# A two-layer DiT in one kernel: opening strips reordered and halved, roots on ScalarE, layer 0's row sums by a matmul with ones, joint and end in half banks

## The chip, the cores and the metric

The kernel runs on one NeuronCore of a Trainium2 chip. The metric is the device time of one execution in microseconds (us). The engines are named as the profile names them: PE (TensorE matmul) and PEld (its weight loads), DVE (VectorE), ACT (ScalarE), POOL (GpSimd), SP (the queue that issues most loads).

## The reference, cut to what matters

Width 2048, 256 tokens of `x` and 256 of `ctx`, all in float32. Layer 0 mixes by a Fourier transform, layer 1 by windowed attention with a prefix; after layer 1 only `x` is kept and normalised once more.

```python
def _rmsnorm(x, g):
    return x * lax.rsqrt(jnp.mean(x * x, axis=-1, keepdims=True) + EPS) * g

for i in range(2):
    shift, scale, gate = split(silu(c) @ ada_w[i] + ada_b[i], 3)         # the same for ctx with c_ctx
    h  = _rmsnorm(x,  norm_g[i]) * (1 + scale)   + shift
    hc = _rmsnorm(xc, norm_g[i]) * (1 + scale_c) + shift_c
    # layer 0: u, z = h @ w_in; y = mix(real(fft2(u))) * silu(z)
    # layer 1: attention over h and hc, y = attention * silu(z)
    x  = x + gate * (y @ w_out[i])
    xc = xc + gate_c * (yc @ w_out[i])                                   # layer 0 only
return _rmsnorm(x, final_g)
```

## The kernel before

Every float32 product is made of three matmuls in a reduced type (`mm3`, lines 74 to 76): both operands are split into a high part (a cast on ACT, line 61) and a low part (a subtraction on DVE, line 62), and high x high, high x low and low x high are added up in PSUM. The small exact products (transposes, the modulation `ada`) are plain float32 matmuls. PSUM has eight banks of 128 x 512. Weights arrive as 128 x 2048 strips of 1 MB through the pool `raw` (three buffers, in the opening two more called `raw2`); SP issues each load as soon as its buffer is free.

**Order of work.** The program text is only a wish. A scheduler lays out the instructions of each engine's queue from estimated times, in the order of the text where it can; `tc.issue_after(ins)` pins what its block issues on the engine of `ins` behind `ins`. The queues are then run in order.

**The opening** (up to about 150 us). The four strips `xn0` to `xn3` are 128 token rows each (two of `x`, two of `ctx`). `square` sums the squares of a strip, half on ACT and half on DVE. `norm(s)` makes the inverse root for two strips (`rsqrt`: scale and offset on DVE, `pow` with exponent -0.5 on POOL, then one Newton step of three DVE operations) and scales the transform's matrix `dm` by it into `dh` and `dl`. `xsplit` splits quarter strips, `dft(s, c)` transforms them on PE (24 matmuls for each of two blocks), `turn_x` transposes strips on PE and `copy_x` takes them out of PSUM. Between them stand the modulation strips: `ada(i, which, kg)` loads one strip of `awp` and multiplies it by the condition vector (line 266), four strips make one row block, `rows_of` copies it out and `turn` transposes it into `gs0` (scale) or `sh0` (shift). In the text before, two of the first eight strips are used before `dft(0, 3)`, four more before `dft(1, 3)`, the last two after it. Then come the gate blocks: for each `i` of four, `z_x` makes the modulated activations (lines 315 to 317) for four `k`, and `z_step(k)` multiplies them by six weight blocks into six PSUM banks, with eight further strips of `ada` between the steps and `z_load`/`z_w` for the weights.

**Layer 0's output and the joint** (about 800 to 1033 us). The loop over `wo0` makes x1 in two sweeps of eight PSUM banks; `evac0(k, o)` takes a bank out (two DVE operations, line 691), squares it on ACT (694) and adds the square to a running sum on DVE (696). Then the rows of x1 are transposed and written out (`x1_turn`), the sums over the partitions are taken by matmuls with one column of ones (748), `rsqrt` makes four roots for each partition, and `bcast_rows` (102) spreads them over all partitions through PE. With them `hx`/`hc` are made (785 to 787), and the k/v products of layer 1 begin.

**The end.** The last output columns are made for row block 0 first and then, from weights held in SBUF, for row block 1. `evac(tb, cb, o)` multiplies by the gate, adds the residual (1094, 1095) and sums squares on ACT (1096); `finish(tb)` makes the root and scales the four column blocks, two on ACT and two on DVE, each followed by its store from SP.

## Time and profile before

| | |
|---|---|
| Median of 3 runs | 1855.57 us (1854.2 to 1858.58) |
| The profiled execution | 1853.97 us, its span 1852.2 us |
| Granted TensorE clock, mean | 0.997 |
| PE busy | 1818.5 us, 98% of the span |
| DVE, ACT, POOL busy | 1411.5, 975.7, 158.7 us |
| Moved by DMA | 362.74 MB, mean 196 GB/s |

A matmul is busy from its issue to its modelled end, and matmuls overlap; so busy time says when PE had nothing to do, and not how quick it was. The span is counted from the first to the last record of the profile; the execution's own time is 1.77 us longer.

### The profile page before, as it was taken

The numbers are of one execution on the slowest core, as the hardware profiler recorded it, in microseconds if no ns is written. First come the engines' busy times: TensorE is split into PE (matmuls) and PEld (weight loads), VectorE is DVE, ScalarE is ACT, GpSimd is POOL, SyncE is SP. The second block draws the span as 40 slices with busy tenths as digits, with TensorE's granted clock in tenths as the row PEclk, the third lists the DMA queues.
The fourth block names the chain that finished last, engine by engine and source line by source line (L and its number), as shares of the span: only waits on it lengthen the run. The fifth ranks groups of instructions, "written<-read, shape, count | busy, mean of one in ns | idle before, by whom it ended". The sixth has DMA issues, their size and how long they took to land.

```text
span 1852.2 us, 26279 instructions
## 1 busy us (share of the span) xinstructions
PE 1818.5 (98%) x9937; PEld 1551.0 (84%) x9937; DVE 1411.5 (76%) x2408; ACT 975.7 (53%) x1715; POOL 158.7 (9%) x182
## 2 busy tenths in 40 slices
PE   8999999999999999999999999999999999999997
PEld 6569999988888888888888787888888888887886
DVE  6658999969797897578964826878878878887454
ACT  6435544534222242214322525888888888896343
POOL 0001000020000000000000001120220220300010
PEclk9999999999999999999999999999999999999999
DMA  8885665476676657564674334334333333435543
GB/s 327 358 352 182 223 204 196 160 266 260 253 278 251 247 212 278 215 234 167 235 271 181 122 107 138 136 114 137 117 134 126 125 131 120 162 134 182 191 173 136
DMA packets 63934, 362.74 MB, mean 196 GB/s; under 512 B 7744, under 2 KB 7888, under 8 KB 29504
## 3 DMA queue, kind: packets, MB, share of 16 engines
q1 hardware_dynamic: 52448, 326.67, 48.7%
q0 software_dynamic: 7472, 27.71, 3.9%
q10 hardware_dynamic: 3888, 6.69, 1.1%
q8 instruction: 78, 1.28, 0.3%
q14 instruction: 48, 0.39, 0.1%
HBM read 346.87 MB, written 14.16 MB: 195 GB/s over the span
## 4 chain that ended last, share of the span: by engine, by line
PE 88%; DMA 3%; DVE 3%; issue 3%; ACT 2%; POOL 0%; ACTq 0%; POOLq 0%; SPq 0%; DVEq 0%
PE ps L75 22%; PE ps L74 22%; PE ps L76 22%; PE ps L967 6%; PE ps L969 3%; PE ps L1023 3%; PE ps L1038 2%; PE ps L1037 2%; PE ps L1003 2%; PE ps L1004 2%; PE ps L266 1%; DMA raw<-in_awp 1%; DMA act<-in_xT 1%; DVE wl L62 1%; DMA raw<-in_adw 1%
## 5 line engine op out<-in xcount | busy, mean ns | idle before, releaser
L61 ACT CAST wh<-raw 128x1024 fp32r<-128x1024 f32 x329 | 344.9, 1051 | 460.5 <-PE ps L75 349.5
L62 DVE TENSOR_TENSOR wl<-raw,wh 128x1024 fp32r<-128x1024 f32 x329 | 416.3, 1268 | 205.8 <-ACT wh L61 200.7
L75 PE MATMUL ps<-act,wh 128*128 128x512 f32 x928 | 361.1, 389 | 0.0
L74 PE MATMUL ps<-act,wh 128*128 128x512 f32 x928 | 357.6, 389 | 0.1
L76 PE MATMUL ps<-act,wl 128*128 128x512 f32 x928 | 356.4, 389 | 0.1
L76 PEld LDWEIGHTS ps<-act,wl 128*128 128x128 f32 x928 | 174.2, 188 | 36.6 <-DVE wl L62 0.5
L75 PEld LDWEIGHTS ps<-act,wh 128*128 128x128 f32 x928 | 174.2, 188 | 36.4 <-DVE act L626 0.2
L74 PEld LDWEIGHTS ps<-act,wh 128*128 128x128 f32 x928 | 174.2, 188 | 36.4 <-ACT act L625 0.5
L967 PE MATMUL ps<-h,wh 128*128 128x512 f32 x512 | 186.9, 400 | 0.0
L596 DVE CUSTOM_DVE_ANT_0 raw<-raw,cb 128x1024 f32<-128x1024 f32 x128 | 155.0, 1221 | 29.9 <-DMA raw<-in_adw 28.9
L596 DVE CUSTOM_DVE_ANT_0 junk<-raw,cb 128x1024 f32<-128x1024 f32 x96 | 117.3, 1221 | 31.4 <-DMA raw<-in_adw 19.3
L969 PE MATMUL ps<-h,wl 128*128 128x256 f32 x512 | 138.1, 280 | 0.0
L75 PE MATMUL ps<-wl,h 128*128 128x512 f32 x320 | 125.7, 393 | 1.5 <-DVE wl L62 1.5
L74 PE MATMUL ps<-wh,h 128*128 128x512 f32 x320 | 124.2, 396 | 0.3 <-ACT h L786 0.3
L76 PE MATMUL ps<-wh,h 128*128 128x512 f32 x320 | 124.1, 391 | 0.0
L967 PEld LDWEIGHTS ps<-h,wh 128*128 128x128 f32 x512 | 96.1, 188 | 18.9
L1005 DVE CUSTOM_DVE_ANT_0 ps<-ps,mask,nsink 128x512 f32<-128x512 f32 x128 | 92.1, 754 | 12.3 <-PE ps L1004 11.3
L1008 ACT ACTIVATE p<-ps,mx 128x512 f32<-128x512 f32 x128 | 87.3, 687 | 24.8 <-DVE mx L1005 24.2
L969 PEld LDWEIGHTS ps<-h,wl 128*128 128x128 f32 x512 | 96.8, 189 | 1.4
L62 DVE TENSOR_TENSOR pl<-ps,ph 128x512 fp32r<-128x512 f32 x128 | 83.7, 685 | 9.8 <-ACT ph L61 8.7
L1013 ACT ACTIVATE p<-p,sm 128x512 f32<-128x512 f32 x128 | 85.5, 717 | 7.8 <-DVE sm L1011 7.8
L75 PE MATMUL ps<-wl,ys 128*128 128x512 f32 x212 | 83.3, 393 | 0.0
(325 smaller groups left out, 3771.6 us busy)
## 6 DMA issues: line engine op xcount, KB each, us to landing
raw<-in_adw SPq DMA_DIRECT2D x64, 1024.0 KB, 5.6
raw<-in_wz SPq DMA_DIRECT2D x62, 1024.0 KB, 4.9
raw<-in_awp SPq DMA_DIRECT2D x32, 1024.0 KB, 7.8
raw<-in_wo SPq DMA_DIRECT2D x32, 1024.0 KB, 5.2
raw<-in_wq SPq DMA_DIRECT2D x32, 1024.0 KB, 4.8
raw<-in_wu SPq DMA_DIRECT2D x25, 1016.0 KB, 5.4
raw<-in_wo1b SPq DMA_DIRECT2D x16, 1024.0 KB, 4.8
act<-in_xT POOLq DMA_DIRECT2D x32, 256.0 KB, 5.6
```

The costliest lines, as they stand in the source:

```text
L61: S.copy(h, src)
L62: V.tensor_tensor(l, src, h.bitcast(F32), op=ALU.subtract)
L74: PE.matmul(o, wh, xh, start=start, stop=False)
L75: PE.matmul(o, wh, xl, start=False, stop=False)
L76: PE.matmul(o, wl, xh, start=False, stop=stop)
L596: V.tensor_tensor_reduce(junk if s == 0 and i < 3 else wf, wf, cb[:, s], 1.0, 0.0, ALU.mult, ALU.add, acc[:, i, kh, fg * 2 + f, s : s + 1])
L967: PE.matmul(o[0], wh[:, q], hx1[k], start=k == 0, stop=k == KT - 1)
L969: PE.matmul(o[0][:, 0:N], wl[:, q], hx1[k][:, 0:N], start=False, stop=False)
L1005: V.tensor_tensor_reduce(o, o, mask[:, tb, :], -0.125, nsink[:, i : i + 1], ALU.add, ALU.min, mx[:, tb : tb + 1])
L1008: S.activation(pt[:, tb, :], so[tb], AF.Exp, bias=mx[:, tb : tb + 1], scale=-1.0, accum_out=sm[:, tb : tb + 1])
L1013: S.activation(pt[:, tb, :], pt[:, tb, :], AF.Copy, scale=sm[:, tb : tb + 1])
L1023: PE.transpose(o[:, (kt * 2 + tb) * P : (kt * 2 + tb + 1) * P], pt[:, tb, c : c + P], ident)
```

## The change

It has four parts.

1. **Opening.** `xn0` and `xn1` are loaded in halves, and their squares are taken in quarters as the halves come (`square(t, n, b)`). `norm(0)` gets a second hook, `under`, for the first PSUM copy, and the low parts `dl` follow it directly. The strips of `ada` move: two before `norm(1)`, all eight of the first two row blocks and two of the next before `dft(1, 2)`; both turns move ahead of `dft(1, 2)`, and the first gate weights are loaded after those strips. In the gate blocks `late`, the second half of `z_step(k + 3)`, is pinned behind the turn's transposes.
2. **Root.** `rsqrt` becomes `root`: ACT takes Sqrt of src/D + EPS, DVE takes the reciprocal, then the same Newton step. One extra Sqrt activation is placed after the first Silu, one in the `wo0` loop and one before the end.
3. **Joint.** The sums over partitions are taken by ones broadcast to 128 columns, so that every partition gets the sum of every token; the root is then taken on 128 x 256 halves. Two of the additions, the first k/v split and the transposes are pinned in an order written out by hand.
4. **End.** The last four blocks of row block 1 are multiplied in two halves of 256 columns; the sums known earlier enter the root through its offset (`known`); one store goes to ACT's queue.

```diff
-    def rsqrt(pool, src, w, tag, between=lambda: None):
-        v = pool.tile([P, w], F32, tag=tag + "v", name=tag + "v")
-        t = pool.tile([P, w], F32, tag=tag + "s", name=tag + "s")
-        r = pool.tile([P, w], F32, tag=tag + "r", name=tag + "r")
-        vi = V.tensor_scalar(v, src, 1.0 / D, EPS, op0=ALU.mult, op1=ALU.add).ins
+    epsd = const.tile([P, 1], F32, name="epsd")
+    GP.memset(epsd, EPS)
+
+    def root(r, v, t, src, bias=None, between=lambda: None):
+        first = S.activation(t, src, AF.Sqrt, bias=epsd if bias is None else bias, scale=1.0 / D).ins
+        vi = V.tensor_scalar(v, src, 1.0 / D, EPS if bias is None else bias, op0=ALU.mult, op1=ALU.add).ins
         with tc.issue_after(vi):
             between()
-        GP.tensor_tensor(r, v, mhalf[:, 0:w], op=ALU.pow)
+        V.reciprocal(r, t)
         V.tensor_tensor(t, r, r, op=ALU.mult)
         V.scalar_tensor_tensor(t, t, -0.5, v, op0=ALU.mult, op1=ALU.mult)
-        V.scalar_tensor_tensor(r, t, 1.5, r, op0=ALU.add, op1=ALU.mult)
-        return r
-
+        return first, V.scalar_tensor_tensor(r, t, 1.5, r, op0=ALU.add, op1=ALU.mult).ins
...
     S.activation(cc, cc, AF.Silu)
+    root_set = const.tile([P, 1], F32, name="root_set")
+    S.activation(root_set, epsd, AF.Sqrt)
...
         for t in range(4):
             xn.append(sx.tile([P, D], F32, name=f"xn{t}"))
-            nc.sync.dma_start(xn[t], a["x2"][t * P : (t + 1) * P])
+            for q in (slice(0, 1024), slice(1024, 2048)) if t < 2 else (slice(0, 2048),):
+                nc.sync.dma_start(xn[t][:, q], a["x2"][t * P : (t + 1) * P, q])
             if t == 1:
                 nc.sync.dma_start(dm, a["dmat"])
...
-        def square(t):
...
+        def norm(s, between=lambda: None, under=lambda: None):
...
             with tc.issue_after(rend[0]) if s else nullcontext():
-                V.tensor_reduce(s2, ss[:, q, :], axis=AX.X, op=ALU.add)
-            r = rsqrt(st, s2, 2, f"r{s}", between)
+                V.tensor_reduce(s2, ss[:, q, 0 : 2 if s else 4], axis=AX.X, op=ALU.add)
+            v, r, t = (st.tile([P, 2], F32, name=f"r{n}{s}") for n in "vrt")
+            chain = root(r, v, t, s2, None, between)[1]
             dh = sx.tile([P, 2, N], F32R, name=f"dh{s}")
             dl = sx.tile([P, 2, N], F32R, name=f"dl{s}")
             for tt in range(2):
                 S.activation(dh[:, tt], dm[:, tt], AF.Copy, scale=r[:, tt : tt + 1])
-                V.scalar_tensor_tensor(dl[:, tt], dm[:, tt], r[:, tt : tt + 1], dh[:, tt].bitcast(F32), op0=ALU.mult, op1=ALU.subtract)
-            rend[0] = V.tensor_copy(rr[:, q], r).ins
+            with tc.issue_after(chain):
+                under()
+            for tt in range(2):
+                rend[0] = V.scalar_tensor_tensor(dl[:, tt], dm[:, tt], r[:, tt : tt + 1], dh[:, tt].bitcast(F32), op0=ALU.mult, op1=ALU.subtract).ins
+            with tc.issue_after(rend[0]):
+                V.tensor_copy(rr[:, q], r)
...
 
...
-                PE.transpose(o2[:, j * P : (j + 1) * P], rows[:, j * P : (j + 1) * P], ident)
+                t_end[0] = PE.transpose(o2[:, j * P : (j + 1) * P], rows[:, j * P : (j + 1) * P], ident).ins
...
         early, late = range(NE // 2), range(NE // 2, NE)
-        square(0)
+        square(0, 4, 0)
+        square(0, 4, 2)
         xsplit(0, 0)
+        square(1, 4, 0)
         xsplit(0, 1)
         ox = turn_x(0, range(8))
-        square(1)
-        norm(0, lambda: xsplit(1, 0))
+        square(1, 4, 2)
+        norm(0, lambda: xsplit(1, 0), lambda: copy_x(0, 0, ox[0]))
         with tc.issue_after(rend[0]):
-            for kp in range(4):
+            for kp in range(1, 4):
                 copy_x(0, kp, ox[kp])
             xsplit(1, 1)
             dft(0, 0)
         xsplit(0, 3)
         xsplit(1, 3)
         ada(0, 1, 0)
+        ada(0, 1, 1)
         norm(1)
         dft(0, 2)
         for t in (2, 3):
             xsplit(t, 0)
-        ada(0, 1, 1)
+        ada(0, 1, 2)
         dft(0, 3)
         for t in (2, 3):
             xsplit(t, 1)
-        for kps in (range(4), range(4, 8)):
+        ada(0, 1, 3)
+        rows = rows_of(1)
+        for c, kps in enumerate((range(4), range(4, 8))):
             ox = turn_x(1, kps)
             for kp in kps:
                 copy_x(1, kp, ox[kp])
+            ada(0, 0, c)
         bcast_rows(rr, r_bc)
-        ada(0, 1, 2)
+        turn(0, 1, rows)
         dft(1, 0)
         for t in (2, 3):
             xsplit(t, 2)
-        ada(0, 1, 3)
-        rows = rows_of(1)
+        ada(0, 0, 2)
+        ada(0, 0, 3)
+        rows = rows_of(0)
         dft(1, 1)
         for t in (2, 3):
             xsplit(t, 3)
-        turn(0, 1, rows)
+        turn(0, 0, rows)
+        ada(1, 1, 0)
+        ada(1, 1, 1)
         wr = z_load(0)
-        ada(0, 0, 0)
         dft(1, 2)
-        ada(0, 0, 1)
         dft(1, 3)
         sta.close()
         wfp = us.enter_context(tc.tile_pool(name="wfp", reuse_waits="tile", bufs=8))
         ch = ub.tile([P, 4, P], F32R, name="ch")
         cl = ub.tile([P, 4, P], F32R, name="cl")
         z_w(0, *wr)
-        ada(0, 0, 2)
-        ada(0, 0, 3)
-        turn(0, 0, rows_of(0))
         for i in range(4):
             k = 4 * i
             for j in range(4):
                 z_x(k + j)
             hx_prep(k)
-            if i < 3:
+            if 0 < i < 3:
                 ada(i + 1, 1, 0)
                 ada(i + 1, 1, 1)
             z_step(k)
                 z_step(k + 3, early)
                 if i < 3:
                     turn(i + 1, 0, rows)
-                z_step(k + 3, late)
+                with tc.issue_after(t_end[0]):
+                    z_step(k + 3, late)
...
-                V.scalar_tensor_tensor(t[:, q], o[:, q], gt0[:, k, s : s + 1], t[:, q], op0=ALU.mult, op1=ALU.add)
...
-            S.activation(t2, t, AF.Square)
-            if 0 < k < 15:
+            with tc.issue_after(kv_w[0]) if k == 8 else nullcontext():
+                sq_end[0] = S.activation(t2, t, AF.Square).ins
+            if k in (13, 14):
+                late.append(t2)
+            elif 0 < k < 15:
                 V.tensor_tensor(sqs[0], sqs[0], t2, op=ALU.add)
             else:
                 sqs.append(t2)
-
+            if k == 15:
+                with tc.issue_after(e):
+                    for t2 in late:
+                        add_end[0] = V.tensor_tensor(sqs[0], sqs[0], t2, op=ALU.add).ins
+
...
+            if i == 31:
+                kv_raw = raw(a["wkv"][0])
+                kv_h = wsp.tile([P, 1024], F32R, tag="ws", name="wh")
+                kv_l = wsp.tile([P, 1024], F32R, tag="ws", name="wl")
+                kv_w.append(S.copy(kv_h, kv_raw[:, 0:1024]).ins)
+            if i == 24:
+                S.activation(junk[:, 0:1], epsd, AF.Sqrt)
...
+    def turns(c, *after):
+        with ExitStack() as es:
+            for i in after:
+                es.enter_context(tc.issue_after(i))
+            for tb in range(2):
+                x1_turn(tb, c)
+
+    p_end = [None]
     o = psum()
-    PE.transpose(o[0:KT, 0:P], gt1.rearrange("p k s -> p (k s)"), ident)
+    p_end[0] = PE.transpose(o[0:KT, 0:P], gt1.rearrange("p k s -> p (k s)"), ident).ins
     gr = const.tile([KT, P], F32, name="gr")
-    S.copy(gr, o[0:KT, 0:P])
+    with tc.issue_after(sq_end[0]):
+        S.copy(gr, o[0:KT, 0:P])
     nc.gpsimd.dma_start(gated.rearrange("o (k p) -> (o k) p", p=P), gr)
-    for c in range(3):
-        for tb in range(2):
-            x1_turn(tb, c)
-    r_bc1 = act()
-    o = psum()
-    for t in range(4):
-        for i in range(2):
-            PE.matmul(o[:, t : t + 1], sqs[i][:, t * P : (t + 1) * P], ones[:, 0:1], start=i == 0, stop=i == 1)
-    r4 = rsqrt(const, o[:, 0:4], 4, "q")
-    bcast_rows(r4, r_bc1)
-    for tb in range(2):
-        x1_turn(tb, 3)
+    for c in range(2):
+        turns(c, sq_end[0], p_end[0])
+    with tc.issue_after(add_end[0]):
+        V.tensor_tensor(kv_l, kv_raw[:, 0:1024], kv_h.bitcast(F32), op=ALU.subtract)
+    r_bc1, qv, qt = act(), act(), act()
+    for s in range(2):
+        q = slice(s * N, (s + 1) * N)
+        o = psum()[:, 0:N]
+        with tc.issue_after(p_end[0]):
+            for i in (1, 0):
+                last = PE.matmul(o, ones[:, 0:1].broadcast_to([P, P]), sqs[i][:, q], start=i == 1, stop=i == 0).ins
+        p_end[0] = last
+        rooted = root(r_bc1[:, q], qv[:, q], qt[:, q], o)[0]
+    for c in range(2, 4):
+        turns(c, p_end[0], rooted)
...
             for kg in range(8):
-                w = ws_split(raw(a["wkv"][kg]))
+                w = [(kv_h, kv_l)] if kg == 0 else ws_split(raw(a["wkv"][kg]))
                 for j in range(2):
                     k = kg * 2 + j
+                    if k == 1:
+                        with tc.issue_after(hx_first):
+                            w.append(half_split(kv_raw, 1))
...
+            def part(tb, j, o):
+                q, t, x = slice(1536 + j * 256, 1792 + j * 256), act()[:, 0:256], x2[tb][3][:, j * 256 : (j + 1) * 256]
+                V.tensor_tensor(t, o, gbc[:, q], op=ALU.mult)
+                V.tensor_tensor(x, x, t, op=ALU.add)
+                S.activation(t, x, AF.Square, accum_out=ss[:, 8 + j : 9 + j])
...
+            def finish(tb, col, base):
+                r, v, t = (fp.tile([P, 1], F32, name=f"f{n}{tb}") for n in "rvt")
+                root(r, v, t, ss[:, col : col + 1], base)
+                for c in (2, 0, 3, 1):
...
+                    (nc.scalar if tb and c == 1 else nc.sync).dma_start(out[tb * P : (tb + 1) * P, c * 512 : (c + 1) * 512], t)
...
             evac(0, 3, o[0])
-            finish(0)
-            for k, w in held:
+            base = [known(tb, 3, ss[:, tb * 4 : tb * 4 + 3], EPS) for tb in range(2)]
+            S.activation(ss[:, 9:10], epsd, AF.Sqrt)
+            finish(0, 3, base[0])
+            for k, w in held[:-4]:
                 step(k, 1, *w)
-            evac(1, 3, o[1])
-            finish(1)
-
+            t, x = act(), x2[1][3]
+            V.tensor_tensor(t, o[1], gbc[:, 1536:2048], op=ALU.mult)
+            V.tensor_tensor(x, x, t, op=ALU.add)
+            for j in range(2):
+                oh = psum()[:, 0:256]
+                for i, (k, (wh, wl)) in enumerate(held[-4:]):
+                    q = slice(j * 256, (j + 1) * 256)
+                    mm3(oh, yh[k][:, P : 2 * P], yh[k][:, N + P : 2 * N], wh[:, q], wl[:, q], i == 0, i == 3)
+                part(1, j, oh)
+                if j == 0:
+                    last = known(1, 1, ss[:, 8:9], base[1][:, 0:1])
+            finish(1, 9, last)
```

More of the change, by code (lines that the diff above doesn't have):

```diff
@@ L194, in tile_dit, with square @@
             xn.append(sx.tile([P, D], F32, name=f"xn{t}"))
-            nc.sync.dma_start(xn[t], a["x2"][t * P : (t + 1) * P])
+            for q in (slice(0, 1024), slice(1024, 2048)) if t < 2 else (slice(0, 2048),):
+                nc.sync.dma_start(xn[t][:, q], a["x2"][t * P : (t + 1) * P, q])
             if t == 1:
                 nc.sync.dma_start(dm, a["dmat"])
-        def square(t):
+        def square(t, n=2, b=0):
+            w = 2048 // n
             for c, f in enumerate((S, V)):
-                dump = wsp.tile([P, 1024], F32, tag="ws", name="dump")
-                x = xn[t][:, c * 1024 : (c + 1) * 1024]
+                dump = wsp.tile([P, 1024], F32, tag="ws", name="dump")[:, 0:w]
+                x = xn[t][:, (b + c) * w : (b + c + 1) * w]
+                o = ss[:, t, b + c : b + c + 1]
                 if f is S:
-                    S.activation(dump, x, AF.Square, accum_out=ss[:, t, c : c + 1])
+                    S.activation(dump, x, AF.Square, accum_out=o)
                 else:
-                    V.tensor_tensor_reduce(dump, x, x, 1.0, 0.0, ALU.mult, ALU.add, ss[:, t, c : c + 1])
-        def norm(s, between=lambda: None):
+                    V.tensor_tensor_reduce(dump, x, x, 1.0, 0.0, ALU.mult, ALU.add, o)
+        def norm(s, between=lambda: None, under=lambda: None):
             q = slice(2 * s, 2 * s + 2)
@@ L259, in tile_dit @@
         ada_end = [None]
+        t_end = [None]
         def ada(i, which, kg):
@@ L698, in evac0 @@
                 sqs.append(t2)
+            if k == 15:
+                with tc.issue_after(e):
+                    for t2 in late:
+                        add_end[0] = V.tensor_tensor(sqs[0], sqs[0], t2, op=ALU.add).ins
+        late, sq_end, add_end, kv_w = [], [None], [None], []
         xin = []
@@ L786, in tile_dit @@
                     S.activation(h[:, 0:N], t[:, q], AF.Identity, bias=sh1[:, k, s : s + 1])
-                    V.scalar_tensor_tensor(h[:, N : 2 * N], t[:, q], sh1[:, k, s : s + 1], h[:, 0:N].bitcast(F32), op0=ALU.add, op1=ALU.subtract)
+                    hx_end = V.scalar_tensor_tensor(h[:, N : 2 * N], t[:, q], sh1[:, k, s : s + 1], h[:, 0:N].bitcast(F32), op0=ALU.add, op1=ALU.subtract).ins
+                if k == 0:
+                    hx_first = hx_end
                 hx1.append(hx)
```

33 lines of the change are left out of this document (17 added, 16 removed).

## The prediction

> **What bounds the kernel now.** I read the page first, then the busy time by stage, then the chain of waits at the stages where TensorE (PE) stands idle. The page's first part:
>
> ```profile
> PE 1818.5 (98%) x9937; PEld 1551.0 (84%) x9937; DVE 1411.5 (76%) x2408; ACT 975.7 (53%) x1715; POOL 158.7 (9%) x182
> ```
>
> PE is busy for 1818.5 of the span's 1852.2 us. The change takes hardly a matmul away, so what can be won lies in the remaining 33.7 us and in the places where PE is busy without being quick. The view of busy time by stretch says where they are (stretch, its length, busy us with instruction counts by engine, granted clock, DMA share, GB/s):
>
> ```profile
> 0.00:16.29 16.29, 7.31 (x36) 6.54 (x36) 8.97 (x22) 9.40 (x17) 2.92 (x11) 1.00 0.90 351
> 50.00:56.00 6.00, 4.43 (x35) 1.72 (x34) 3.32 (x9) 4.15 (x10) 0.00 (x0) 1.00 0.84 314
> 73.00:87.00 14.00, 11.10 (x74) 5.42 (x67) 7.47 (x25) 4.99 (x13) 0.00 (x0) 1.00 1.01 421
> 129.00:137.00 8.00, 6.30 (x35) 4.12 (x32) 3.45 (x11) 1.71 (x4) 0.00 (x0) 1.00 0.89 371
> 150.00:1021.00 871.00, 870.48 (x4751) 760.11 (x4750) 716.19 (x1085) 313.97 (x481) 40.52 (x75) 1.00 0.63 229
> 1021.00:1033.00 12.00, 9.42 (x62) 8.56 (x61) 7.03 (x16) 7.97 (x16) 1.54 (x2) 0.86 0.66 209
> 1840.00:1852.00 12.00, 0.71 (x4) 0.23 (x2) 3.32 (x9) 2.06 (x4) 0.56 (x1) 0.68 0.34 113
> ```
>
> PE idles 8.98 us before 16.29, then 1.57, 2.90 and 1.70 us in three short stretches of the opening; 2.58 us in the joint between the layers, at a clock of 0.86; 11.3 us at the end. From 150 to 1021 it idles half a microsecond. The change works in the opening, the joint and the end, and I cost those; the long middle only shifts.
>
> **The opening, four terms.** The chain of waits of the first 18 us (start, length, what; lines between left out):
>
> ```profile
> 1.18 5.15 DMA xn<-in_x
> ...
> 9.33 1.14 DVE dump L206
> ...
> 10.59 0.17 DVE s L212
> ...
> 11.11 1.02 POOL r0r L85
> ...
> 12.54 0.17 DVE r0r L88
> ...
> 12.82 1.28 DVE act L256 x2
> 14.10 0.60 DVE xs L62
> 14.70 1.14 DVE dump L206
> ...
> 15.84 0.41 DVE dl L218
> ...
> 16.29 0.39 PE ps L75
> ...
> 17.16 0.12 PE ps L74
> ```
>
> *First start.* The second strip's square on DVE ends at 10.47, the root is ready at 12.71 by way of POOL, and PE runs steadily only from 16.29, because `dl` stands on DVE behind two PSUM copies (1.28), a split (0.60) and a square of the third strip (1.14). After: the first strip lands at 6.33 as now and the second, 1 MB at the 421 GB/s above, 2.5 later, near 8.9; in halves only a 512-wide square (half of 1.14, 0.6) follows it: sum at 9.75. The root is then one ACT Sqrt (0.25, an estimate from the 0.17 of the small DVE rows), a reciprocal and three small DVE operations of 0.2 each: 11.05, or 11.7 if the split of `between` (0.60) stands ahead of the reciprocal; I take 11.7, 1.0 earlier. `dl` then follows one copy: ready 1.15 after the root instead of 3.5. PE runs from 12.85, and of the 3.44 us it had used 0.5 (four matmuls at 0.12): -2.9; I take -2.7. Bounds: -1.0 (root earlier, `dl` as late as now) to -3.4.
>
> *Start of the gate blocks (50 to 56).* Two rows of the groups (operation, count | busy, mean ns | idle before) price what stands there:
>
> ```profile
> L316 ACT ACTIVATE ext<-act,sh 128x256 fp32r<-128x256 f32 x32 | 13.6, 496 | 14.7 <-DVE sh L281 14.7
> L61 ACT CAST ext<-raw 128x512 fp32r<-128x512 f32 x8 | 4.7, 617 | 0.4 <-DMA raw<-in_wz 0.4
> ```
>
> L316 waits for the shift `sh`, which is now turned before `dft(1,3)`. That wait goes. But the two strip products that covered the start have moved ahead as well: a copy, two casts and two of L316 (about 2.4 us overlapped) stand bare unless the strips of `ada(1,1,2)` and `(1,1,3)` are in and fill it. Between -1.2 and +0.8: -0.6, as the strips should be in, next.
>
> *Strip waits (73 to 87).* DMA runs at 421 GB/s there: strips are late. Earlier it stood still for want of free buffers:
>
> ```profile
> 30.00:35.00 5.00, 5.00 (x46) 3.40 (x45) 4.44 (x7) 5.00 (x9) 0.00 (x0) 1.00 0.13 23
> 45.00:50.00 5.00, 5.00 (x42) 4.03 (x41) 2.27 (x6) 1.76 (x3) 0.00 (x0) 1.00 0.72 264
> ```
>
> The new order uses ten strips before the gate blocks instead of six before `dft(1,3)`, so buffers come free sooner; filling the first stretch alone moves 4.3 us of transfer forward. Of the 2.90 us of idle I take -1.0 (0 to -2.9), since the later loads still wait for the gate weights' splits.
>
> *Last block (129 to 137).* `late` (9 matmuls of 0.23, 2.0 us) is now pinned behind the turn's transposes and covers mod, shift and L316: -1.2 (0 to -1.7). What PE then waits for, the row copy, is covered by `early`.
>
> The Sqrt table that is loaded early costs nothing where it stands: ACT has nothing to do until the first strip is in, and the load back to Silu falls before the gate outputs, where ACT waits for PE. Moving z_load behind ten strips on SP's queue puts it behind some 16.5 MB, at 421 GB/s near 43 us; the gate start lies at 50. Opening: **-5.5**.
>
> **The joint.** The chain there, with the DVE row that follows it and the clock of the gap:
>
> ```profile
> 1022.57 1.23 DVE wl L62
> 1023.80 0.61 DVE act L696
> 1024.41 0.04 issue
> 1024.45 1.96 PE ps L748 x16
> ...
> 1026.68 1.04 POOL qr L85
> ...
> 1028.45 2.04 PE ps L102 x8
> ...
> 1032.43 0.50 PE ps L74
> ```
> ```profile
> 1031.15 1.67 DVE L785 SCALAR_TENSOR_TENSOR ht<-act,gs 128x256 f32<-128x256 f32 x4 [2.85 <-ACT act L103]
> ```
> ```profile
> 1028.00:1030.00 2.00, 1.55 (x7) 1.58 (x8) 0.27 (x2) 0.00 (x0) 0.00 (x0) 0.61 0.93 296
> ```
>
> From the finished sum (1024.41) to layer 1's first matmul takes 8.0 us. After: evacuation ends at 1022.5 as now; two held adds (0.61 each) give the sum at 1023.75; the k/v split pinned behind them holds DVE to 1024.9, and under it run the ones products, which fill all partitions at once, and ACT's Sqrt. Then DVE does ten 128x256 operations; four take 1.67, so 0.41 each: 4.1 us, to 1029.0. From L785 to the matmul stays 1.28 (1031.15 to 1032.43): 1030.3. That is -2.1; I take **-2.0**. The unknown price is a 128x256 reciprocal; its nearest wide rows are those L785, 0.41. Bounds: -3.3 if the split falls behind the root, -0.5 if hand-offs add 0.15 to each of the ten. The extra Sqrt loads (one in the wo0 loop, where ACT idles) are off the path. Queued behind the pinned split on DVE is the root itself, hence the 1.14 counted.
>
> **The end.** The view in order of time:
>
> ```profile
> 1840.75 0.69 DVE L1094 TENSOR_TENSOR act<-ps,gbc 128x512 f32<-128x512 f32 x1 [3.42 <-PE ps L76]
> 1842.20 0.63 ACT L1096 ACTIVATE act<-act 128x512 f32<-128x512 f32 x1 [4.63 <-DVE act L1095]
> 1843.38 0.56 POOL L85 TENSOR_TENSOR f1r<-f1v,mhalf 128x1 f32<-128x1 f32 x1 [7.82 <-DVE f1v L82]
> 1844.56 1.33 ACT L1135 ACTIVATE act<-act,f1r 128x512 f32<-128x512 f32 x2 [1.63 <-DVE f1r L88]
> ```
>
> Four blocks in halves: 24 matmuls of 0.12 for 12 of 0.23, +0.1. Two DVE operations at half width: -0.55; the square -0.2; Sqrt and reciprocal (0.45) for reduce, scale and pow (1.0): -0.55. Outputs start with the short operation, and one is issued from ACT: -0.2. Sum **-1.4**, bounds -0.8 to -2.0. The Sqrt load stands eight matmul groups before it is needed.
>
> **Sum.** -5.5 - 2.0 - 1.4 = -8.9. The profiled execution took 1853.97 us, 1.77 more than its span, and lies 1.6 under the median of 1855.57; against the median the sum gives **1846.7**. With every term at its end it would be -1.5 or -14.5; they don't all fall together, so the forecast's own range is 1842.5 to 1850.5.
>
> **Rivals.** *A slow reciprocal.* DVE's cost for one element:
>
> ```profile
> L62 DVE TENSOR_TENSOR wl<-raw,wh 128x1024 fp32r<-128x1024 f32 x329 | 416.3, 1268 | 205.8 <-ACT wh L61 200.7
> L1011 DVE RECIPROCAL sm<-sm 128x2 f32<-128x2 f32 x64 | 10.5, 165 | 1.8
> ```
>
> 1268 ns for 1024 elements and 0.41 us for 256 make about 1.1 ns an element. The only reciprocal in the trace is two wide, 165 ns, which tells little: eight passes would add 15 ns. If it took eight, 256 elements cost 2.1 us, two halves 3.4 more than counted, and PE, which has products and transposes to about 1027, would wait some 6 us for the k/v products instead of 3. A shorter, thin stretch already brought the clock to 0.61 (above); 4 us of k/v at 0.61 would cost 1.6. Together +5.0: 1851.7. Against: nothing but the short row. Chance 0.24.
> The Trainium skill, VectorE: DVE Perf Modes, section "First, the fixed hardware budget", says that Reciprocal is an iterative divide with a repeat count of 8; no row here is wide enough to show it. For the second half of this rival, TensorE: Matmul & The Clock Gate, "What's actually happening", puts the clock at half after an idle window of about 3.4 us, and the trace's 0.61 agrees.
>
> *The opening is bound by its transfers.* PE's earlier start is waited away at the strips, DMA being at 0.90 and 1.01 in two of the stretches. For it: those rows; against: the idle DMA from 30 to 50. Opening -1.5 instead of -5.5: 1850.7. Chance 0.09.
>
> *Slower: ACT tables that share nothing.* If Sqrt's table lacks Square, Copy or Identity, each root reloads twice on the path.
>
> ```profile
> L115 ACT ACT_TABLE_LOAD x1 | 1.3, 1283 | 1.7 <-PEq L1261 1.7
> L1008 ACT ACT_TABLE_LOAD x1 | 1.3, 1283 | 0.0
> ```
>
> Two loads serve the whole run now, and the squares of L1096 run after the second without one, which speaks against it. Price: two loads at each of two opening norms and the final one, four in the joint with its copies: ten of 1.28, 12.8 us: 1859.5. It decides from seven such loads on. Chance 0.05.
>
> *No effect:* the order on each queue is laid out from estimated times, and may have been nearly this already; 1855.6. Chance 0.06.
>
> **How the numbers follow.** Forecast 0.56. About 0.2% (3.7 us) is what a measurement of this kernel can tell from no change, so faster means under 1851.9: 0.55 of the forecast, 0.12 of the slow reciprocal, 0.07 of the bound opening: 0.74. Same: 0.01, 0.11, 0.02, and 0.05 from the last two: 0.19. Slower: 0.07, the tables mostly. The range reaches from 1842 to 1853.5, past the slow reciprocal; outside stay the tables, no effect and the tails, 0.19.
>
> **What would show it.** Right: steady DFT matmuls from about 13 us; no idle over 1 us from 50 to 140; the first k/v matmul 9 us, not 11, after the last of layer 0; root ready 2.6 us after PE's last matmul instead of 3.8. Wrong: RECIPROCAL of 128x256 near 2 us; more than six ACT_TABLE_LOADs; a gate start with 2 us of bare PE; strips still waited for at 70 to 90.

## The result, and the profile after

| kernel | median | runs | ratio to the kernel before |
|---|---|---|---|
| before | 1856.42 us (1854.06 to 1858.58) | 22 | 1 |
| after | 1852.99 us (1850.35 to 1857.07) | 22 | 0.9983, 95% interval 0.9977 to 0.9990 |

The change makes the kernel faster, by 3.4 us in the medians; forecast were 8.9. The interval excludes a ratio of 1, but the 3.4 us stay under the 3.7 that the prediction named as the least it could tell from no change. The profiled execution after took 1852.08 us, its span is 1850.3 us. The first part of its page, beside the one shown of before:

```profile
PE 1817.7 (98%) x9933; PEld 1550.2 (84%) x9933; DVE 1418.7 (77%) x2429; ACT 984.6 (53%) x1733; POOL 154.6 (8%) x178
```

The view of busy time by stretch, for most of the stretches that the prediction quoted:

```profile
0.00:16.29 16.29, 9.33 (x53) 8.92 (x54) 9.17 (x26) 11.40 (x24) 1.92 (x11) 1.00 0.88 331
50.00:56.00 6.00, 4.88 (x40) 3.09 (x32) 3.31 (x4) 5.01 (x9) 0.00 (x0) 1.00 0.89 331
73.00:87.00 14.00, 14.00 (x80) 8.54 (x73) 8.95 (x36) 7.14 (x16) 0.00 (x0) 1.00 0.95 365
129.00:137.00 8.00, 8.00 (x39) 6.56 (x38) 5.19 (x13) 5.37 (x12) 0.00 (x0) 1.00 0.51 189
1021.00:1033.00 12.00, 5.74 (x28) 4.81 (x29) 10.46 (x19) 7.38 (x15) 0.05 (x1) 0.85 0.47 175
```

The opening's rows went the forecast way: PE does 2.02 us more before 16.29, and its idle time from 73 to 87 (2.90) and from 129 to 137 (1.70) is gone from these stretches. The joint went the other way: from 1021 to 1033 PE is busy 5.74 us, where it was 9.42. Layer 0 ends 3 us earlier here, so the same part of the stage lies from 1018 to 1030; from 1017.8 to 1029.8 PE is busy 6.37. The view of PE's waits names what is left, in us in total, times and the longest:

```profile
PE ps L74 <- ACT h L828: 6.3, 1, 6.3
PE ps L74 <- ACT ext L326: 2.3, 1, 2.3
PE ps L276 <- DMA raw<-in_awp: 1.8, 1, 1.8
```

L828 is the joint, L326 the start of the gate blocks; the waits for modulation strips (`in_awp`) were 3.2 us in four and are 1.8 in one.

**The joint.** DVE in order of time (start, busy us, line, operation; in brackets the idle time before it):

```profile
1019.36 1.48 DVE L720 TENSOR_TENSOR act<-act 128x512 f32<-128x512 f32 x2
1020.75 1.22 DVE L783 TENSOR_TENSOR wl<-raw,wh 128x1024 fp32r<-128x1024 f32 x1
1023.51 0.42 DVE L83 TENSOR_SCALAR act<-ps 128x256 f32<-128x256 f32 x1 [1.54 <-ACT act L82]
1023.85 1.74 DVE L86 RECIPROCAL act<-act 128x256 f32<-128x256 f32 x1
1025.51 0.36 DVE L83 TENSOR_SCALAR act<-ps 128x256 f32<-128x256 f32 x1
1025.79 1.74 DVE L86 RECIPROCAL act<-act 128x256 f32<-128x256 f32 x1
1027.44 0.69 DVE L87 TENSOR_TENSOR act<-act 128x256 f32<-128x256 f32 x2
1028.05 0.75 DVE L88 SCALAR_TENSOR_TENSOR act<-act 128x256 f32<-128x256 f32 x2
1028.72 0.75 DVE L89 SCALAR_TENSOR_TENSOR act<-act 128x256 f32<-128x256 f32 x2
1029.39 1.67 DVE L827 SCALAR_TENSOR_TENSOR ht<-act,gs 128x256 f32<-128x256 f32 x4
```

A reciprocal of 128x256 takes 1.74 us, four to five times the 0.35 to 0.42 of the other root operations of its size. PE meanwhile has run out of transposes, and then runs slowly:

```profile
1020.22 2.23 PE L790 MATMUL ps<-act,ones 128*128 128x256 f32 x8
1022.29 1.91 PE L761 MATMUL ps<-ident,act 128*128 128x128 f32 x16
1030.46 0.79 PE L74 MATMUL ps<-wh,h 128*128 128x512 f32 x1 [6.26 <-ACT h L828]
1031.06 0.63 PE L75 MATMUL ps<-wl,h 128*128 128x512 f32 x1
1031.48 0.63 PE L74 MATMUL ps<-wh,h 128*128 128x512 f32 x1
```
```profile
1030.00:1036.00 6.00, 5.54 (x13) 4.37 (x14) 6.00 (x12) 3.46 (x7) 0.00 (x0) 0.50 0.24 63
```

The first matmuls of layer 1 come some 0.43 us apart (1031.06, 1031.48), where before they came 0.23 apart, and the stretch from 1030 to 1036 has a granted clock of 0.50. The rows of before:

```profile
1032.77 0.40 PE L75 MATMUL ps<-wl,h 128*128 128x512 f32 x1
1033.00 0.39 PE L74 MATMUL ps<-wh,h 128*128 128x512 f32 x1
```

From the end of layer 0's output (the transpose of the gate, which follows its last matmul) to the first k/v matmul it is 11.1 us before (1021.36 to 1032.43) and 12.1 after (1018.37 to 1030.46).

**The stages of every profile.** The starts of four operations divide each execution: the first gate output (a, from the span's start), the last evacuation of layer 0, the first softmax reciprocal (c, from the mark before it: joint and the k/v work), and the first square of the output block (e, from there to the span's end). Of the two stretches left over, that from the first gate output to the last evacuation varies by 2.3 us over all profiles, that between c and e by 0.4.

| profile of | opening a | joint c | end e |
|---|---|---|---|
| before | 150.1 | 142.9 | 142.5 |
| after | 146.4 | 146.9 | 140.1 |
| joint back | 150.1 | 143.3 | 140.4 |
| opening only | 150.2 | 143.3 | 142.4 |
| joint only | 153.0 | 146.7 | 142.4 |
| end only | 154.5 | 142.5 | 140.2 |

Joint and end repeat well: the new joint takes 145.8 to 147.0 us in five profiles (mean 146.5; three of them are of experiments below), the old one 142.5 to 143.3 in four (143.0), so it costs 3.5; the new end brings 2.2. The opening doesn't repeat: 150.1 to 154.5 for the old text (mean of three 152.5), 146.4 to 150.2 for the new (mean of six 148.5), with the same order of the opening's instructions on PE, ACT, DVE and the load queue. So one profile can't price the opening, and the forecast's four terms were taken from one.

### The profile page after: what moved, and what is told of

The parts are those of the page before. It is cut to its first block, busy times and chain, and to the rows that moved or that the text cites. A ratio compares the mean times of both kernels' runs of the same rounds, so it can differ in the third digit from the quotient of the medians.

```text
span 1850.3 us, 26316 instructions
## 1 busy us (share of the span) xinstructions
PE 1817.7 (98%) x9933; PEld 1550.2 (84%) x9933; DVE 1418.7 (77%) x2429; ACT 984.6 (53%) x1733; POOL 154.6 (8%) x178
## 3 DMA queue, kind: packets, MB, share of 16 engines
q8 instruction: 78, 1.28, 0.3%
## 4 chain that ended last, share of the span: by engine, by line
PE 93%; DVE 2%; ACT 2%; DMA 1%; issue 1%; POOL 0%; SPq 0%; ACTq 0%; DVEq 0%; POOLq 0%
PE ps L74 24%; PE ps L75 24%; PE ps L76 24%; PE ps L1014 6%; PE ps L1016 3%; PE ps L1070 3%; PE ps L1085 2%; PE ps L1084 2%; PE ps L1050 2%; PE ps L1051 2%; PE ps L276 1%; DVE wl L62 1%; DMA raw<-in_awp 0%; ACT wh L61 0%; DMA act<-in_xT 0%
## 5 line engine op out<-in xcount | busy, mean ns | idle before, releaser
L75 PE MATMUL ps<-wl,ys 128*128 128x512 f32 (+1 forms) x216 | 84.0, 389 | 0.0
```

The source lines that it names most:

```text
L75: PE.matmul(o, wh, xl, start=False, stop=False)
```

## The experiments

**One part alone, and the joint undone.** First the joint is put back (the old sums, `rsqrt` and `bcast_rows`, and the old order without pins; opening and end as changed):

```diff
-    for s in range(2):
...
-                last = PE.matmul(o, ones[:, 0:1].broadcast_to([P, P]), sqs[i][:, q], ...)
+    for t in range(4):
+        for i in range(2):
+            PE.matmul(o[:, t : t + 1], sqs[i][:, t * P : (t + 1) * P], ones[:, 0:1], ...)
+    r4 = rsqrt(const, o[:, 0:4], 4, "q")
+    bcast_rows(r4, r_bc1)
```

> The change with the joint of before: column sums, the small root by way of POOL, and the broadcast through PE; opening and end stay changed. Theory A (the joint lost what the opening won: the 128x256 reciprocals take 1.74 us each, and the long gap lets the clock fall): without them the opening's 3.0 us and the end's 2.4 are left whole, 5.4 under before, about 1851.0 where the change has 1853.0; at 1034 to 1036 the granted clock is 1.00 again. Rival B (the joint is neutral and the opening's lead is lost elsewhere): no gain on the change, 1853.

Measured: 1850.66 us, 0.9971 (0.9962 to 0.9981). Without the new joint the change gains more; by the medians' ratios 2.2 us more, by the stages 3.6. Then each part alone, by the same hunks:

> Before with only the opening of the change (halved strips, moved modulation strips, the root on ACT there, late pinned). If the ledger of the two traces holds, 2.6 to 3.7 under before: about 1853.2, and the first gate evacuation near 146.4 instead of 150.1. If the lead of the opening is taken back by what follows it (transfers of the next stage), under 1 us.

> Before with only the joint of the change. Theory A: 3.5 slower than before, about 1859.9, RECIPROCAL 128x256 at 1.74, the clock near 0.5 at the start of k/v. Rival B (the joint is neutral): within 1 us of before.

> Before with only the end of the change. By the traces 2.4 under before, 1854.0 (forecast 1.4): root 2.55 us after PE's last matmul instead of 3.8, and the stores started earlier and on two queues. Rival: the stores bound the end and only 1.2 is left.

Measured: opening alone 0.9987 (0.9978 to 0.9996), joint alone 1.0026 (1.0016 to 1.0037), end alone 0.9998 (0.9989 to 1.0007). The joint alone makes the kernel slower: that sign is settled. Of 1856 us these are -2.4, +4.8 and -0.4, each uncertain by nearly 2 us; they add up to +2.0, and the whole change gave -3.2. The opening alone (2.6 to 3.7 us expected) and the end alone (2.4) came out lower than expected. The end alone shows 2.2 us less in its stage but not in its total; its profiled opening took 154.5 us on an unchanged order, which hides the gain in that execution, but whether the other runs met such openings isn't shown. What stays open is whether the parts really help one another or whether eight to eleven runs of each met different openings.

**The price of the wide reciprocal.** The two 128x256 reciprocals become a linear operation of the same size, so the joint's factor is not a root in this kernel and only its time counts:

```diff
-        V.reciprocal(r, t)
+        if r.shape[-1] > 4:
+            V.tensor_scalar(r, t, -1.0, 2.0, op0=ALU.mult, op1=ALU.add)
+        else:
+            V.reciprocal(r, t)
```

> The change with the two wide reciprocals replaced by one multiply-and-add of the same size (2 - t; the root of the joint is then not a root, and the output not the reference's). Theory A: each drops from 1.74 to about 0.41 us, the first k/v matmul comes 2.7 us earlier, and with a gap of 3.6 instead of 6.3 us the clock may stay up, another 2.5: 1848 to 1850.3. This is the joint as the prediction priced it. Rival B (the chain is held by something else, the pinned split or the transposes): within 0.5 us of the change, 1852.5 to 1853.5.

Measured: 1849.7 us, 0.9968 (0.9956 to 0.9980), stage c 142.7, 3.8 under the new joint's mean. DVE and PE in its profile:

```profile
1026.12 0.42 DVE L83 TENSOR_SCALAR act<-ps 128x256 f32<-128x256 f32 x1 [1.53 <-ACT act L82]
1026.47 0.28 DVE L87 TENSOR_SCALAR act<-act 128x256 f32<-128x256 f32 x1
```
```profile
1030.29 0.80 PE L74 MATMUL ps<-wh,h 128*128 128x512 f32 x1 [3.47 <-ACT h L831]
```

0.28 us in place of 1.74, twice, is 2.9 us. PE's wait shrinks by that (6.26 to 3.47), and the clock recovers sooner. The wait of 1.53 for the sums and ACT's Sqrt ahead of the root stays.

This is the joint nearly as the prediction priced it, and it still doesn't bring its -2.0. The first k/v matmul comes 9.3 us after layer 0's output (1020.98 to 1030.29), 1.8 earlier than before, but then the clock is 0.50 and 0.70 for 4 us; stage c is 142.7 against the old joint's 143.0.

**The clock by itself.** 26 matmuls whose result is overwritten fill the wait, so that PE stays busy while the reciprocals run as changed:

```diff
+            o = [[psum() for _ in range(2)] for _ in range(4)]
+            with tc.issue_after(p_end[0]):
+                for _ in range(26):
+                    PE.matmul(o[3][1], kv_h[:, 0:P], kv_h[:, 0:512], start=True, stop=True)
...
-            o = [[psum() for _ in range(2)] for _ in range(4)]
```

> The change with 26 added 128x512 matmuls on PE, 5.9 us by 0.227, in the gap between the last transposes and the first k/v product; their result is written over by the k/v products. The wide reciprocals stay. Theory A: the clock stays at 1.00 and the first 14 k/v matmuls take 3.2 instead of 5.8 us: 2.5 less, 1850.5. Rival C (layer 1's start is paced by DVE's activations, the clock costs nothing): within 0.5 us of the change.

Measured: 1850.79 us, 0.9975 (0.9966 to 0.9985), stage c 144.2, 2.3 under the new joint's mean. The first products start 0.23 apart again:

```profile
1024.62 6.15 PE L824 MATMUL ps<-wh 128*128 128x512 f32 x26
1031.13 0.50 PE L74 MATMUL ps<-wh,h 128*128 128x512 f32 x1 [0.36 <-ACT h L832]
1031.47 0.40 PE L75 MATMUL ps<-wl,h 128*128 128x512 f32 x1
1031.70 0.40 PE L74 MATMUL ps<-wh,h 128*128 128x512 f32 x1
```

The first k/v matmul comes 12.1 us after layer 0's output, as in the kernel after, so the filling shifts nothing ahead of it; what it changes is the clock, 1.00 throughout. So the new joint loses in two ways, and filling the wait takes one of them back: about 2.3 us of half clock. The rest, 1.2 us against the old joint's 143.0, agrees with the first k/v matmul coming 1.0 later than before (12.1 for 11.1). Both figures come from one profile of this kernel.

**The small root on the new order.** Column sums, a root by Sqrt and reciprocal on 128x4, then `bcast_rows`; the pinned order and the held additions stay:

```diff
-                last = PE.matmul(o, ones[:, 0:1].broadcast_to([P, P]), sqs[i][:, q], ...)
+                last = PE.matmul(o[:, t : t + 1], sqs[i][:, t * P : (t + 1) * P], ones[:, 0:1], ...)
...
+    rooted = root(r4, v4, t4, o[:, 0:4])[0]
...
+        bcast_rows(r4, r_bc1)
```

> The change with its pinned order, but with column sums and the root by Sqrt and reciprocal on 128x4, then the broadcast through PE as before. Theory A: 1.96 for the column sums, 1.2 for the small root, 1.5 for broadcast and copy instead of 8.6 from the sum to the activations: the first k/v matmul 3 us earlier, and a gap of PE under 2 us, so at full clock: 5 to 6 under the change, 1847 to 1848. Rival B: 1852.5 to 1853.5.

Measured: 1850.56 us, 0.9970 (0.9960 to 0.9980), stage c 142.4. The narrow reciprocal:

```profile
1023.92 0.17 DVE L86 RECIPROCAL qr<-qt 128x4 f32<-128x4 f32 x1
```
```profile
1029.25 0.50 PE L74 MATMUL ps<-wh,h 128*128 128x512 f32 x1 [1.74 <-ACT h L830]
```

0.17 us against 3.48, and the transposes and the products that spread the root keep PE at work: its wait is 1.74 us. The gain of 2.4 us on the change is half of the 5 to 6 expected. The two later profiles with this root gave 144.1 and 144.7 for stage c, with waits of 1.81 and 2.75; in all three the clock falls to 0.50, in different stretches between 1022 and 1034. The mean of the three, 143.7, is about the old joint's 143.0. Held additions, pinned split and Sqrt on ACT win nothing that these profiles show.

**Whole strips instead of halves.** The first two loads are made whole again, the squares stay in quarters:

```diff
-            for q in (slice(0, 1024), slice(1024, 2048)) if t < 2 else (slice(0, 2048),):
+            for q in (slice(0, 2048),):
```

> The change with the first two strips loaded whole again; the squares stay in quarters. Theory D (the half loads share the engines and do not arrive early: the last half of the second strip came at about 10.2 where the whole strip had come at 8.97): the second strip is there by 9.0, the sum at 10.2 instead of 11.25, PE steady from 13 instead of 14: 1 us under the change, 1852.0. Rival E (halves arrive earlier as planned, and the root is late for want of DVE): 1 us over the change or the same.

Measured: 1852.08 us, 0.9981 (0.9972 to 0.9989), no difference from after, where 1 us was expected. When the strips come in is shown by the rows that wait for them, first in halves, then whole:

```profile
6.29 0.63 ACT L208 ACTIVATE dump<-xn 128x512 f32<-128x512 f32 x1 [1.59 <-DMA xn<-in_x]
8.83 0.63 ACT L208 ACTIVATE dump<-xn 128x512 f32<-128x512 f32 x1 [0.16 <-DMA xn<-in_x]
10.23 0.69 DVE L210 CUSTOM_DVE_ANT_0 dump<-xn 128x512 f32<-128x512 f32 x1 [0.15 <-DMA xn<-in_x]
```
```profile
6.50 0.63 ACT L208 ACTIVATE dump<-xn 128x512 f32<-128x512 f32 x1 [1.79 <-DMA xn<-in_x]
9.09 0.63 ACT L208 ACTIVATE dump<-xn 128x512 f32<-128x512 f32 x1 [0.23 <-DMA xn<-in_x]
13.73 0.39 PE L75 MATMUL ps<-dl,xs 128*128 128x256 f32 x1
```

A half strip is there at 6.29, hardly before the whole one (6.35 before the change, 6.50 here), and the last half of the second strip only at 10.23, where the whole strip was in at 8.99 and 9.09. Over all profiles the first half comes at 5.5 to 6.6 (mean of ten 5.9) and the whole strip at 6.35 to 6.8 (mean of four 6.6); the last half of the second strip comes at 9.9 to 10.9 (10.2), the whole at 9.0 to 9.4 (9.2). So the first half gains 0.7 us and the last, on which the root depends, loses 1.0. Steady PE starts at 13.73 with whole strips and at 13.98 with halves. The halves bring nothing.

**The start of the gate blocks.** In five of the seven profiles with the new opening taken so far the clock falls to 0.50 right after PE's 2.32 us wait for ACT's L326, which is there in all seven. The profile with the opening alone:

```profile
56.00:58.00 2.00, 0.86 (x3) 0.77 (x4) 2.00 (x6) 2.00 (x6) 0.00 (x0) 0.94 1.10 271
58.00:60.00 2.00, 2.00 (x6) 1.54 (x6) 2.00 (x10) 2.00 (x6) 0.00 (x0) 0.50 0.91 369
60.00:62.00 2.00, 2.00 (x8) 1.58 (x7) 2.00 (x9) 1.80 (x4) 0.00 (x0) 0.71 1.00 397
```

The profile of after is one of the two without that drop, which flattered its opening; the other, that of the linear operation, has one at 128 to 132, behind a wait of 2.63 us for a strip. Two kernels take the wait away. One fills it with six matmuls, the other gives the cover back:

```diff
-                zo.extend(psum() for _ in range(NE))
+                zo.extend(psum() for _ in range(NE)); g = dd[1][0].rearrange("p a b -> p (a b)"); [PE.matmul(zo[NE - 1], g[:, 0:P], g, start=True, stop=True) for _ in range(6)]
```

> Adds six matmuls (128x512, their result is overwritten) on PE ahead of the first gate block, 1.4 us of work inside the 2.32 us in which PE waits for ACT's first ext there (changed kernel). Theory, the clock step: in five of seven profiles with the new opening the granted clock falls to 0.50 at 58 us, right after that wait; with the wait cut to about 0.9 us the clock should stay at 1.00 from 56 to 62, the first gate evacuation should come at 146 to 147 (149.0 to 150.1 and 147.5 to 150.2 with the drop), and the time should be 1 to 2 us under the changed kernel's 0.9983 of the kernel before: 0.9972 to 0.9978. Rival, the strips decide: what the clock loses at 58 is waited for anyway at the strips between 73 and 87, and the time stays at 0.9983.

```diff
-        ada(1, 1, 0)
-        ada(1, 1, 1)
         wr = z_load(0)
...
         z_w(0, *wr)
+        ada(1, 1, 0)
+        ada(1, 1, 1)
```

> The two strips of ada(1,1,0) and ada(1,1,1) go back behind the first gate weights, as cover for the gate start, all else as changed. Theory, bare gate start: PE's wait at 55 to 57 falls from 2.32 us to 1.2 or less, the clock stays at 1.00 from 56 to 62, the strip waits behind it stay near 3 us; 1.5 to 2.5 us under the changed kernel: 0.9970 to 0.9975 of the kernel before. Rival, the strips come too late: their products aren't there to cover the start, the wait turns from ACT to DMA, and the time stays at 0.9983 or rises to 0.9990.

Measured: filled 1851.51 us, 0.9978 (0.9967 to 0.9989), stage a 146.4; covered 1850.29 us, 0.9967 (0.9954 to 0.9979), stage a 143.6. PE at the gate start, after, filled and covered:

```profile
53.81 1.06 PE L276 MATMUL ps<-raw,c 128*32 128x512 f32 x8
57.20 0.50 PE L74 MATMUL ps<-ext,wh 128*128 128x512 f32 x1 [2.32 <-ACT ext L326]
```
```profile
55.10 1.06 PE L276 MATMUL ps<-raw,c 128*32 128x512 f32 x8
57.10 0.73 PE L74 MATMUL ps<-ext,wh 128*128 128x512 f32 x2 [0.94 <-ACT ext L326]
```
```profile
51.34 2.78 PE L276 MATMUL ps<-raw,c 128*32 128x512 f32 x24
54.72 1.20 PE L74 MATMUL ps<-ext,wh 128*128 128x512 f32 x4 [0.60 <-ACT ext L326]
56.00:62.00 6.00, 6.00 (x31) 4.09 (x29) 6.00 (x25) 5.62 (x12) 0.00 (x0) 1.00 0.97 381
```

What starts the gate blocks is the chain on ACT behind the last transform's copy: two casts, L344 twice, L326. From that copy to PE's first matmul it takes 3.28 us in both orders (53.92 to 57.20, and 51.44 to 54.72). A strip's product is eight records of PE, 1.06 us. In the changed order two strip products have been done before the transform ends, and one strip (1.06 us) is left to lie over the chain; in the covered order all three strips (2.78 us) lie over it, the transform itself ends 2.5 us earlier, and the gate starts at 54.72. The covered kernel's gain over after (0.9983 to 0.9967, 3 us) comes with both the wait and the drop gone; the filled one's 1 us lies within its interval.

**Both repairs together.** The small root with either repair of the gate start, by the edits above:

> The small root at the joint (128x4, measured 0.9970 of the kernel before) with the six matmuls ahead of the first gate block. If joint and gate start add: 0.9959 to 0.9965, first gate evacuation at 146 to 147, joint 142.4 from the last evacuation of layer 0 to the first softmax reciprocal. If the strips decide: 0.9970 as without the matmuls.

> The small root at the joint with the two strips put back behind the first gate weights. If joint and gate start add: 0.9957 to 0.9965; PE's wait at 55 to 57 at 1.2 us or less. If the strips come too late to cover: 0.9970 to 0.9977.

Measured: 1849.19 us, 0.9964 (0.9952 to 0.9977), with the filled wait; 1847.85 us, 0.9954 (0.9941 to 0.9966), with the cover. The second beats both the kernel before, by 8.0 us in the medians, and the change, by about 5; that the small root adds to the cover isn't resolved (0.9967 and 0.9954, with intervals that overlap). In none of the four profiles with a filled or covered gate start does the clock in the opening fall below 0.99 in any stretch of 2 us.

## Why the prediction was right or wrong

The direction was right, but the size of the forecast was wrong: -3.4 us instead of -8.9. The median of 1852.99 lies outside the forecast's own range (1842.5 to 1850.5) and inside the wide one only because that reached past the slow reciprocal. By the means of the stages the ledger is: opening -4.0 for -5.5, joint +3.5 for -2.0, end -2.2 for -1.4. That is -2.7 for the -3.4 of the medians; the opening's spread is larger than what is missing.

*The joint is the step that failed.* Its term priced the reciprocal of 128x256 at 0.41 us "by its nearest wide rows". It takes 1.74; the two alone are 2.7 us over the sum. The other eight operations took less than 0.41, so that the ten together took 5.88 us (1023.51 to 1029.39) where 4.1 were counted. The term called this price unknown, but its lower bound (-0.5) was built from hand-offs and left it out, although the rival had it: 2.1 us by eight passes (its own 1.1 ns an element would give 2.25), PE waiting some 6 us, and 4 us of k/v at a reduced clock. That rival's time was 1851.7, 1.3 us from the result. Its mechanism is what the runs show: PE waited 6.26 us, the reciprocal took 1.74, and the clock cost 2.3 where 1.6 were priced; that its total came so close is in part luck, since opening and end, which it took over from the forecast, missed by 1.5 and 0.8 in opposite directions. A second error: the ones products and ACT's Sqrt were said to run under the split, but DVE waited 1.54 us for them, since a cast of weights and a copy stood ahead of the Sqrt on ACT (1021.59 to 1023.11). A third: the half clock was left out of the likeliest case. The filled wait puts 2.3 us on it. The three close the account of the joint: 1.8 for the root, 1.5 for the wait and 2.3 for the clock are 5.6, and from -2.0 to +3.5 it is 5.5. With the reciprocals gone the whole loss is gone, since the wait shrinks with them, but the forecast's gain still doesn't come: what the earlier start brings, the clock takes back.

On the reciprocal, what the prediction quoted from the Trainium skill, VectorE: DVE Perf Modes, "First, the fixed hardware budget" (a repeat count of 8), points the right way: 256 elements less the 0.17 us of a narrow operation leave 1.57 us, 6.1 ns an element, about five and a half times the forecast's 1.1. On the clock, the Trainium skill, TensorE: Matmul & The Clock Gate, "What's actually happening", speaks of a free-running window of about 3.4 us; that it runs free fits a drop in five of seven profiles with one start of the gate blocks, but the wait there was only 2.32 us long. The 0.61 in which the prediction saw agreement came behind a wait of 2.05 us (PE's row of L102, the products that spread the root), so it fits the half clock and not that length. Nor does the longest wait alone decide: 0.94 and 0.60 at the gate start were followed by no drop in two profiles each, but a drop came in the end-only kernel at 78 to 82, where PE did only strip products with waits of 0.47 and 1.43, and in the small root's at 1022 to 1028, where it did only transposes and one-column sums with a wait of 0.35. What decides there stays open.

*First start.* The reordered `dl` did what was said: ready directly after one copy, and steady PE 2.31 us earlier (16.29 to 13.98) for 2.7. But the other half of that term was wrong:

```profile
11.25 0.16 DVE L216 TENSOR_REDUCE s<-ss 128x2 f32<-128x8 f32 x1 [0.32 <-ACT dump L208]
12.71 0.16 DVE L89 SCALAR_TENSOR_TENSOR rr<-rt,rr 128x2 f32<-128x2 f32 x1
13.44 0.89 DVE L226 SCALAR_TENSOR_TENSOR dl<-dm,rr,dh 128x256 fp32r<-128x256 f32 x2
```

The sum, forecast for 9.75, came at 11.25, and the root was ready at 12.87 where it had been at 12.71. The second strip's last half landed late (10.23), and the sum waited for ACT's last square, which stood behind two casts (9.46 to 10.58); with whole strips, the second in at 9.09, the sum came at 11.00 all the same. The forecast had left the casts out. (Its root at 11.05 doesn't come out of its own terms either: 9.75, 0.25 and four of 0.2 are 10.8.) The gain is all `dl`.

*Start of the gate blocks.* -0.6 was chosen "as the strips should be in", with +0.8 as the other bound. In the profile the wait was 2.32 us where PE had idled 1.57 (+0.75); the chain on ACT, put at 2.4, took 3.28. In five of seven profiles half clock came on top, which the term didn't have: 56 to 62 at a mean of 0.72 in the profile of the opening alone would be 1.7 us at most, an estimate. Named as cover and then allowed to go: the sentence on what costs if that cover is gone was right, the choice between the ends wasn't.

*Strip waits and last block.* Right: 3.2 us of strip waits fell to 1.8 (3.2 to 5.2 in three profiles of the old order, 0.7 to 3.2 in six of the new), and 129 to 137 has no idle time left (8.00 of 8.00). *z_load behind ten strips* showed in no wait for a transfer between 30 and 62.

*The end.* Right, under-priced. Each step is in the rows of DVE and ACT:

```profile
1841.26 0.42 DVE L1147 TENSOR_TENSOR act<-ps,gbc 128x256 f32<-128x256 f32 x1 [0.53 <-PE ps L76]
1842.72 0.29 ACT L82 ACTIVATE ft<-ss,ku 128x1 f32<-128x1 f32 x1
1843.05 0.16 DVE L86 RECIPROCAL fr<-ft 128x1 f32<-128x1 f32 x1
1843.83 1.34 ACT L1194 ACTIVATE act<-act,fr 128x512 f32<-128x512 f32 x2 [0.81 <-DVE fr L89]
```

From the last evacuation's start to the first output of ACT was 3.81 us (1840.75 to 1844.56) and is 2.57 (1841.26 to 1843.83). That is 1.24; the other 1 us of the stage was not separated.

*Other rivals.* ACT's tables: there are six loads of 1.28 us for two before, none of the four added stands on the path, and no Square or Copy between them brought a further one, so Sqrt's table serves them here as well. Transfers as the bound: PE's earlier start was not waited away at the strips, whose waits fell, and the covered kernel, with the same strips to load, has an opening of 143.6.

*The signs.* Of those that the prediction named, steady transform matmuls came at 13.98 for 13, and the root at the end 2.6 us after PE's last matmul, as forecast. The first k/v matmul came 12.1 us after layer 0's output for 9, the reciprocal was near 2 us, and PE stood bare for 2.3 us at the gate start: these were its signs of being wrong.

That the forecast's opening was to be had is shown by the covered kernels: their last evacuation of layer 0 starts at 1016.8 and 1018.4, before at 1022.2 (and at 1024.9 and 1027.1 in the other two profiles with the old opening). With the end's -2.2 and a joint that costs nothing this gives -6 to -7.6 beside the one profile before; the kernel with both repairs measured -8.0.

## What to carry to other kernels

Price an operation that no trace shows at the width at which it will be used, and let the likeliest case carry the doubt: a reciprocal on four columns and a spread through TensorE cost less than the same reciprocal on every partition and token. When work is moved, ask what it was covering: here two strip products of about 1 us each stood over a chain of 3.3 us on ACT, and without them PE waited 2.3 us and in most profiles lost clock behind it. And when a stage differs by several microseconds between executions of one order, take its price from several profiles.

## What the runs showed of the hardware

- A DVE reciprocal took 0.16 to 0.17 us for 128x1 to 128x4 and 1.74 us for 128x256, where multiplications and additions of that size took 0.28 to 0.42.
- Waits of PE of 2.32 us were followed by a granted clock of 0.50 for some 3 us in five of seven profiles, a wait of 3.47 by 0.50 and 0.70 for 4 us, one of 6.26 by 0.50 for 6 us. Stretches of strip products, transposes or one-column sums with waits of at most 1.43 and 0.35 us also ended at 0.50.
- Two 512 KB loads for one of 1 MB on one queue: the first half landed at 5.9 us in the mean of ten profiles (6.6 as a whole, mean of four), the second strip's last half at 10.2 (9.2 as a whole).
- The same queue orders gave openings of 150.1, 153.0 and 154.5 us. The last had the clock at 0.50 in two places, 18 to 20 and 80 to 82. The second had no such drop, but waited 5.2 us for strips where the first waited 3.2.
